# Projection steps of the next head pair, three per query block in the even head, and a fifth buffer for the first exponentials

## Chip, core and metric

The kernel runs on one core of a Trainium2 chip. The metric is the device time of one execution in microseconds (us). The engines are named as the profile names them: PE is TensorE's matmul, PEld its weight load, DVE is VectorE, ACT is ScalarE, POOL is GpSimd and SP issues most of the DMAs.

## What is computed

Two residual layers over 512 tokens of width 1024 in float32, each followed by a SwiGLU feed-forward. Layer 0 mixes tokens by stick-breaking attention, layer 1 by differential attention. The change lies in layer 1; cut to what matters, it is:

```python
def diff_mixer(h, positions, w_in, w_out, q_g, k_g, ..., sub_g, layer_idx):
    q, k, v = split(h @ w_in, 3)                  # 8 heads; q and k in 2 halves of 64, v of 128
    q, k = rms_norm(q, q_g), rms_norm(k, k_g)     # over each 64
    q1, q2, k1, k2 = partial_rope(...)            # the first 16 of each 64
    a = softmax(mask(q1 k1^T)) - lam * softmax(mask(q2 k2^T))
    o = rms_norm(a @ v, sub_g) * (1 - lam_init)   # per head
    return o @ w_out
```

## The kernel before

Activations are kept transposed, as eight tiles of 128 features by 512 tokens. Every matmul operand is split into a high and a low part, so one product is three matmuls (lines 216, 217 and 218). Layer 1's attention is `diff_layer`.

**Chunks and heads.** Heads go in pairs. Chunk c projects q, k and v of heads 2c and 2c+1. `qk_steps(c)` makes a tile of 512 columns for each of four token blocks in two steps each (8 steps of 12 matmuls of 512 columns), and `v_steps(c)` a tile of 256 columns in one step each (4 steps of 24 matmuls of 256 columns): 12 steps for a chunk. After its last block `qk_steps` normalises the whole chunk (L766 to L769) and applies the rotary part (L786 to L789). Each block's square (L758) goes to a scratch tile `tmp`, of which there are three, and so do the scratch of the rotary part and the square of `head_out` (L861).

**One head.** `head_stacks` transposes q and k of a head (L798) and splits them (L311 to L315; k's halves are doubled by a DMA from POOL, L334). `attend` then goes through four query blocks, the longest first: `weights(3)`, `weights(2)`, a bank of transposes (L358, then L361 and L362), `weights(1)`, a bank, `weights(0)`, a bank. `weights` makes two sets of scores (L340, L341), the maximum (L811), two exponentials (L812, tiles `e1` and `e2`) and combines them into `e1` (L824). All four `e1` tiles of a head are read by its last bank of transposes. Then `head` multiplies by v (tile `av`, L216 to L218), and `head_out` norms the head's output: L850, transposes L856 (`tn`), squares L861, the scaling L874, transposes L883 (`tb`) and the split L886, L887 into two tiles of pool `hp`. `head_out` of one head is called by the next one, after its `weights(3)`.

**Fillers.** The steps of chunks 1 to 3 stand in a queue; `attend` takes `counts[hd]` steps from it at four places of a head. In the middle of an odd head the rest of the next chunk's q and k is taken from the queue, and then `head_stacks` of the following head is called. From head 6 on, the queue holds `out_first`, which needs the outputs of heads 0 to 3 only; `out_second` needs those of heads 4 to 7 and follows the last head.

**What sets the order.** The kernel is built with `schedule_with_timeline_sim=True`: the build plays the program through in simulated time and writes each engine's queue in the order in which instructions became ready there, the earlier one in the program first where several are ready. So a filler step stands at one place in the program and may be run at another. Tiles of one tag take its buffers by turns, in program order. The rings that matter: `tmp` 3, `e1` 4, `e2` 2, scores in PSUM 2, projection tiles in PSUM (`mm`) 2, `wt_hi`/`wt_lo` 1, q2 and k2 stacks 2 each, v 2, pool `hp` 26 (the layer's input takes 16 of these, each head's output two).

Of the kernel before, what the change touches and what calls it, by code (L numbers as in the profile page):

```python
# [12 lines left out]
F32 = mybir.dt.float32  # L13
# [8 lines left out]
P = 128  # L22
S = 512
# [8 lines left out]
ROT = 16  # L32
RSQRT_MAGIC = float(0x5F3759DF)
TCK = dict(schedule_with_timeline_sim=True)
HP = 26
WB = 5
THIRDS = ((0, 8), (8, 8), (16, 6))
TWO_PI_A = 6.28125
# [5 lines left out]
def trunk(  # L44
# [30 lines left out]
    xp = ctx.enter_context(tc.tile_pool(name="xp", bufs=1))  # L75
    hp = ctx.enter_context(tc.tile_pool(name="hp", bufs=HP))
    wp = ctx.enter_context(tc.tile_pool(name="wp", bufs=WB))
# [199 lines left out]
    def out_first(layer, og):  # L277
        for g in range(4):
            w = out_load(layer, 0, g)
            for mi in range(2):  # L280
                m = g * 2 + mi
                ps = mm.tile([P, S], F32, tag="mm", name="ps_o")
                out_mms(ps, w, og, range(4), mi, 0, 3)
                V.tensor_tensor(x[m], x[m], ps, op=ALU.add)
                yield
# [51 lines left out]
    def scores(ps, q2, k2, e, qt):  # L337
        n = max(2, qt + 1) * P
        qs = slice(qt * P, (qt + 1) * P)
        T.matmul(ps[:, :n], q2[:, e, qs], k2[:, 0, e, :n], start=True, stop=False)  # L340
        T.matmul(ps[:, :n], q2[:, e, qs], k2[:, 1, e, :n], start=False, stop=True)  # L341
# [365 lines left out]
    def diff_layer(norm, nxt):  # L707
        h = norm.h
        with ExitStack() as st:
# [3 lines left out]
            at = st.enter_context(tc.tile_pool(name="at1", bufs=2))  # L713
# [88 lines left out]
            def weights(q2, k2, ss, qt):  # L802
                n = (qt + 1) * P
                nm = sm.tile([P, 2], F32, tag="nm", name="nm")
                e1 = at.tile([P, S], F32, tag="e1", bufs=4, name="e1")
                e2 = at.tile([P, S], F32, tag="e2", name="e2")
                for e, o in ((0, e1), (1, e2)):
                    ps = scp.tile([P, S], F32, tag="sc", name="sc")
                    scores(ps, q2, k2, e, qt)
                    V.memset(ps[0:64, n - 64 : n], NEG)  # L810
                    V.reduce_max(nm[:, e : e + 1], ps[:, :n], axis=AX.X, negate=True)  # L811
                    A.activation(  # L812
                        o[:, :n],
                        ps[:, :n],
                        AF.Exp,
                        bias=nm[:, e : e + 1],
                        accum_out=ss[:, e, qt : qt + 1],
                    )
                c = sm.tile([P, 2], F32, tag="c", name="c")
                V.reciprocal(c[:, 0:1], ss[:, 1, qt : qt + 1])  # L820
                V.tensor_scalar(
                    c[:, 1:2], ss[:, 0, qt : qt + 1], nlam, c[:, 0:1], op0=ALU.mult, op1=ALU.mult
                )
                V.scalar_tensor_tensor(  # L824
                    e1[:, :n], e2[:, :n], c[:, 1:2], e1[:, :n], op0=ALU.mult, op1=ALU.add
                )
                return e1

            def head(hh, q2, k2, v, after, middle, steps, before):
                ss = sm.tile([P, 2, TT], F32, tag="s12", name="s12")  # L830
                attend(tpp, wts, lambda qt: weights(q2, k2, ss, qt), after, middle, steps)
                before()
                v = v()
                av = avp.tile([P, S], F32, tag="av", name="av")
                hs = slice(hh * P, (hh + 1) * P)
                for kt in range(TT):
                    n, hi, lo = wt_chunk(wts, kt)
                    mm3(
                        av[:, :n],
                        (v[0][:, kt, hs], v[1][:, kt, hs]),  # L840
                        (hi, lo),
                        kt == 0,
                        kt == TT - 1,
                    )
                return av, ss
# [58 lines left out]
                gens["v", c] = v_steps(c, vs)  # L904
                fillers.extend((gens["qk", c], gens["v", c]))
            last = out_first(1, og)
            counts = ((2, 1, 2, 1), (2, 1, 1, 1)) * 3 + ((1, 1, 1, 1), (1, 1, 1, 1))
            for hd in range(8):
                hh = hd % 2
                c = hd // 2  # L910
# [32 lines left out]
    assert not todo  # L943
    n3 = Norm(gf, KT, True)
    diff_layer(n2, n3)
    ffn(1, n3, store)

# [72 lines left out]
```

## Time and profile before

| | before |
|---|---|
| median of 3 runs | 1301.82 us (1300.54 to 1305.36) |
| the profiled execution: its time | 1301.36 us |
| its span | 1299.6 us |
| PE busy | 1239.7 us (95%) |
| DVE busy | 740.2 us (57%) |
| ACT busy | 568.2 us (44%) |
| POOL busy | 80.8 us (6%) |
| chain that ended last, by engine | PE 90%, DVE 3%, ACT 3%, DMA 2% |

The page's second part cuts the span into 40 slices of 32.5 us. Layer 1's attention lies between about 640 and 931 us, slices 20 to 29. A head is recognised in the trace by its twelve `av` matmuls; the ends of these give the stretches in the rows below.

### The profile page before, as it was taken

The numbers are of one execution on the slowest core, as the hardware profiler recorded it, in microseconds if no ns is written. First come the engines' busy times: TensorE is split into PE (matmuls) and PEld (weight loads), VectorE is DVE, ScalarE is ACT, GpSimd is POOL, SyncE is SP. The second block draws the span as 40 slices with busy tenths as digits, with TensorE's granted clock in tenths as the row PEclk, the third lists the DMA queues.
The fourth block names the chain that finished last, engine by engine and source line by source line (L and its number), as shares of the span: only waits on it lengthen the run. The fifth ranks groups of instructions, "written<-read, shape, count | busy, mean of one in ns | idle before, by whom it ended". The sixth has DMA issues, their size and how long they took to land.

```text
span 1299.6 us, 16000 instructions
## 1 busy us (share of the span) xinstructions
PE 1239.7 (95%) x5974; PEld 1032.3 (79%) x5974; DVE 740.2 (57%) x1426; ACT 568.2 (44%) x964; POOL 80.8 (6%) x132
## 2 busy tenths in 40 slices
PE   6999999889999999999999997968899999999998
PEld 5888888778888888888888887745688888888886
DVE  5567868597544554455535657677754434443442
ACT  7777887455332432334324445345443223321220
POOL 1211111000000000000000000000000000000000
PEclk8999999999999999999999998979899999999999
DMA  7965768238776777766557352501222323332222
GB/s 222 220 148 134 169 143 191 58 97 275 247 227 244 242 246 231 243 233 227 196 194 227 131 158 90 174 17 33 97 100 97 95 97 98 98 97 97 93 73 77
DMA packets 61133, 199.44 MB, mean 153 GB/s; under 512 B 8320, under 2 KB 9344, under 8 KB 61056
## 3 DMA queue, kind: packets, MB, share of 16 engines
q1 hardware_dynamic: 42768, 140.74, 33.0%
q0 software_dynamic: 18144, 57.68, 16.8%
q8 instruction: 47, 0.77, 0.2%
q14 instruction: 30, 0.25, 0.1%
q10 hardware_dynamic: 144, 0.01, 0.0%
HBM read 154.36 MB, written 35.65 MB: 146 GB/s over the span
## 4 chain that ended last, share of the span: by engine, by line
PE 90%; DVE 3%; ACT 3%; DMA 2%; issue 1%; SPq 0%; POOL 0%; DVEq 0%; ACTq 0%; POOLq 0%
PE ps_d L217 6%; PE ps_d L216 6%; PE ps_d L218 6%; PE ps_g L218 6%; PE ps_g L216 6%; PE ps_g L217 6%; PE ps_u L218 6%; PE ps_u L216 6%; PE ps_u L217 6%; PE ps_nat L216 4%; PE ps_nat L217 4%; PE ps_nat L218 4%; PE ps_o L216 2%; PE ps_o L217 2%; PE ps_o L218 2%; PE tp L358 2%
## 5 line engine op out<-in xcount | busy, mean ns | idle before, releaser
L109 ACT ACTIVATE whi<-wraw 128x1024 fp32r<-128x1024 f32 (+1 forms) x136 | 138.6, 1033 | 355.8 <-PE ps_d L217 82.4
L110 DVE TENSOR_TENSOR wlo<-wraw,whi 128x1024 fp32r<-128x1024 f32 (+1 forms) x136 | 161.9, 1192 | 106.1 <-ACT whi L109 50.5
L217 PE MATMUL ps_d<-alo,whi 128*128 128x512 f32 x352 | 139.1, 396 | 0.0
L218 PE MATMUL ps_d<-ahi,wlo 128*128 128x512 f32 x352 | 139.0, 396 | 0.0
L216 PE MATMUL ps_d<-ahi,whi 128*128 128x512 f32 x352 | 138.9, 396 | 0.0
L216 PE MATMUL ps_u<-hhi,whi 128*128 128x512 f32 x352 | 137.7, 391 | 0.3 <-DVE x L298 0.2
L218 PE MATMUL ps_g<-hhi,wlo 128*128 128x512 f32 x352 | 137.6, 391 | 0.0
L217 PE MATMUL ps_g<-hlo,whi 128*128 128x512 f32 x352 | 137.2, 390 | 0.0
L218 PE MATMUL ps_u<-hhi,wlo 128*128 128x512 f32 x352 | 137.1, 390 | 0.0
L217 PE MATMUL ps_u<-hlo,whi 128*128 128x512 f32 x352 | 137.1, 390 | 0.0
L216 PE MATMUL ps_g<-hhi,whi 128*128 128x512 f32 x352 | 136.7, 390 | 0.0
L217 PE MATMUL ps_nat<-wlo,hhi 128*128 128x256 f32 (+1 forms) x384 | 124.7, 325 | 7.0 <-DMA wlo<-in_wv 7.0
L216 PE MATMUL ps_nat<-whi,hhi 128*128 128x256 f32 (+1 forms) x384 | 124.5, 326 | 1.1 <-DVE k L453 1.0
L218 PE MATMUL ps_nat<-whi,hlo 128*128 128x256 f32 (+1 forms) x384 | 124.7, 325 | 0.0
L606 DVE TENSOR_TENSOR x<-x,ps_d 128x512 f32<-128x512 f32 x48 | 32.8, 687 | 97.2 <-PE ps_d L218 97.1
L217 PEld LDWEIGHTS ps_nat<-wlo,hhi 128*128 128x128 f32 x384 | 74.1, 193 | 12.5 <-DMA wlo<-in_wv 7.2
L216 PEld LDWEIGHTS ps_nat<-whi,hhi 128*128 128x128 f32 x384 | 74.0, 193 | 7.0 <-DVE k L453 1.2
L217 PEld LDWEIGHTS ps_d<-alo,whi 128*128 128x128 f32 x352 | 66.2, 188 | 15.9
L218 PEld LDWEIGHTS ps_d<-ahi,wlo 128*128 128x128 f32 x352 | 66.2, 188 | 15.9
L216 PEld LDWEIGHTS ps_d<-ahi,whi 128*128 128x128 f32 x352 | 66.2, 188 | 15.9
L218 PEld LDWEIGHTS ps_nat<-whi,hlo 128*128 128x128 f32 x384 | 74.1, 193 | 5.1 <-issue 0.2
L216 PEld LDWEIGHTS ps_u<-hhi,whi 128*128 128x128 f32 x352 | 66.1, 188 | 14.9 <-ACT whi L109 0.6
(206 smaller groups left out, 2328.5 us busy)
## 6 DMA issues: line engine op xcount, KB each, us to landing
wraw<-in_wgu SPq DMA_DIRECT2D x88, 512.0 KB, 3.6
wraw<-in_wd SPq DMA_DIRECT2D x32, 512.0 KB, 3.6
k<-k POOLq DMA_DIRECT2D x32, 256.0 KB, 3.3
praw<-in_wqk SPq DMA_DIRECT2D x16, 512.0 KB, 5.7
kept_wqk<-whi POOLq DMA_DIRECT2D x16, 512.0 KB, 5.5
kept_wqk<-wlo POOLq DMA_DIRECT2D x16, 512.0 KB, 6.6
whi<-kept_wqk SPq DMA_DIRECT2D x16, 512.0 KB, 6.3
wlo<-kept_wqk SPq DMA_DIRECT2D x16, 512.0 KB, 5.9
```

The source lines that it names most:

```text
L109: A.activation(hi[:, :cols], raw[:, :cols], AF.Copy)
L110: V.tensor_tensor(lo[:, :cols], raw[:, :cols], hi.bitcast(F32)[:, :cols], op=ALU.subtract)
L216: T.matmul(ps, lh[0], rh[0], start=first, stop=False)
L217: T.matmul(ps, lh[0], rh[1], start=False, stop=False)
L218: T.matmul(ps, lh[1], rh[0], start=False, stop=last)
L358: T.transpose(tp[:, o : o + P], w[qt][:, kt * P : (kt + 1) * P], ident)
L606: V.tensor_tensor(x[m], x[m], ps, op=ALU.add)
```

## The change

```diff
-HP = 26
+HP = 25
...
             def weights(q2, k2, ss, qt):
                 n = (qt + 1) * P
                 nm = sm.tile([P, 2], F32, tag="nm", name="nm")
-                e1 = at.tile([P, S], F32, tag="e1", bufs=4, name="e1")
+                e1 = at.tile([P, S], F32, tag="e1", bufs=5, name="e1")
...
-            counts = ((2, 1, 2, 1), (2, 1, 1, 1)) * 3 + ((1, 1, 1, 1), (1, 1, 1, 1))
+            counts = ((3, 3, 3, 3), (0, 0, 0, 0)) * 3 + ((1, 1, 1, 1), (1, 1, 1, 1))
```

Before, six steps are taken in an even head and five in an odd one, so the last steps of a chunk spill into the odd head and, from there, into the next even head. After the change the even head 2c takes all 12 steps of chunk c+1 and the odd head takes none. `e1` has five buffers instead of four, and pool `hp` 25 tiles instead of 26 (a tile of either is 2 KB per partition). No instruction is added or removed.

## Rows read from the trace of the kernel before

**Rows 1.** The page, parts 1 and 2: engines, and PE's clock by slice
```profile
PE 1239.7 (95%) x5974; PEld 1032.3 (79%) x5974; DVE 740.2 (57%) x1426; ACT 568.2 (44%) x964; POOL 80.8 (6%) x132
PEclk8999999999999999999999998979899999999999
```

**Rows 2.** Busy by stretch: length, PE, PEld, DVE, ACT, POOL, clock, DMA, GB/s
```profile
721.70:743.60 21.90, 21.90 (x134) 19.39 (x134) 14.70 (x56) 9.59 (x27) 0.00 (x0) 1.00 0.50 181
743.60:788.10 44.50, 44.50 (x273) 39.72 (x272) 25.58 (x73) 20.86 (x55) 2.31 (x4) 1.00 0.53 171
788.10:802.50 14.40, 8.85 (x38) 6.71 (x36) 12.52 (x52) 7.07 (x24) 0.00 (x0) 0.64 0.00 1
802.50:846.20 43.70, 39.62 (x214) 32.58 (x214) 32.00 (x87) 18.44 (x49) 2.32 (x4) 1.00 0.45 145
846.20:863.30 17.10, 11.27 (x44) 7.85 (x43) 15.24 (x62) 7.58 (x25) 0.00 (x0) 0.70 0.01 1
863.30:894.60 31.30, 20.91 (x89) 15.24 (x88) 22.55 (x68) 16.44 (x45) 2.31 (x4) 0.84 0.17 34
894.60:905.90 11.30, 9.12 (x51) 6.85 (x50) 8.29 (x36) 5.99 (x21) 0.00 (x0) 1.00 0.12 26
905.90:931.00 25.10, 19.60 (x76) 15.42 (x75) 13.61 (x30) 12.21 (x24) 0.00 (x0) 0.80 0.22 74
```

**Rows 3.** PE in order of time: scores at two head boundaries (start, length)
```profile
728.40 0.28 PE L341 MATMUL sc<-k,q 128*128 128x256 f32 x1
...
751.61 0.39 PE L340 MATMUL sc<-k,q 128*128 128x512 f32 x1
...
839.36 0.28 PE L341 MATMUL sc<-k,q 128*128 128x256 f32 x1
...
840.90 0.50 PE L340 MATMUL sc<-k,q 128*128 128x512 f32 x1 [0.93 <-ACT e L812]
```

**Rows 4.** ACT in order of time: chunk 1's last block and head 0's squares
```profile
694.42 0.69 ACT L756 ACTIVATE qk_nat<-ps_nat,rstd 128x512 f32<-128x512 f32 x1
...
727.67 0.37 ACT L861 ACTIVATE o_sq<-tn,rs 128x128 f32<-128x128 f32 x1
...
728.01 0.64 ACT L758 ACTIVATE qk_sq<-qk_nat 128x512 f32<-128x512 f32 x1
```

**Rows 5.** DVE in order of time: chunk 1's norm
```profile
733.92 2.28 DVE L769 TENSOR_TENSOR qk_nat<-qk_nat,rs_u 128x2048 f32<-128x2048 f32 x1
```

**Rows 6.** ACT in order of time: the first two v blocks of chunk 3
```profile
802.44 0.84 ACT L735 ACTIVATE v1h<-ps_nat,rsv 128x256 fp32r<-128x256 f32 x2 [2.12 <-PE av L217]
```

**Rows 7.** ACT in order of time: an exponential of head 1's first block
```profile
713.19 0.69 ACT L812 ACTIVATE e<-sc,nm 128x512 f32<-128x512 f32 x1 [0.21 <-PE tp L358]
```

**Rows 8.** Groups of DVE by form, 689 to 906 us: count, busy us, mean ns
```profile
L811 DVE TENSOR_REDUCE nm<-sc 128x1 f32<-128x512 f32 x16 | 10.9, 689 | 0.4
L315 DVE SCALAR_TENSOR_TENSOR q<-tqk,gqT,q 64x512 fp32r<-64x512 f32 x14 | 10.5, 750 | 7.0 <-ACT q L314 6.5
L312 DVE TENSOR_TENSOR k<-tqk,k 64x512 fp32r<-64x512 f32 x14 | 9.6, 684 | 2.4 <-ACT k L311 2.0
L824 DVE SCALAR_TENSOR_TENSOR e<-e,c,e 128x512 f32<-128x512 f32 x8 | 5.9, 742 | 0.3
```

**Rows 9.** PE in order of time: matmuls of chunk 0's projections
```profile
654.72 0.39 PE L217 MATMUL ps_nat<-wlo,hhi 128*128 128x512 f32 x1
...
657.66 0.39 PE L218 MATMUL ps_nat<-whi,hlo 128*128 128x512 f32 x1
657.89 0.28 PE L216 MATMUL ps_nat<-whi,hhi 128*128 128x256 f32 x1
...
669.28 0.28 PE L218 MATMUL ps_nat<-whi,hlo 128*128 128x256 f32 x1
```

**Rows 10.** DVE and PE in order of time, layer 0: pair 4's output, last projection
```profile
187.05 0.69 DVE L533 TENSOR_TENSOR olo<-o,ohi 128x512 fp32r<-128x512 f32 x1
...
190.67 0.39 PE L216 MATMUL ps_k<-hhi,whi 128*128 128x512 f32 x1
```

## Prediction

> **What bounds the kernel now.** The page comes first: PE is busy for 95% of the span, and its clock is full except in the first slice and in slices 25 to 29 [rows 1]. So the rest of the kernel has little to give, and I look at layer 1's attention alone, by stretches that end with each head's product with v [rows 2]. The reader should see two halves. Up to 788.1 (the end of head 2) PE is busy without a gap at full clock. From there on it isn't: head 3 takes 14.4 us with PE busy 8.85 at clock 0.64, and heads 4 to 7 take 43.7, 17.1, 31.3 and 11.3 us, 103.4 in all, with PE busy 80.9. DVE is busy for 12.52 of head 3's 14.4 us (87%) and 15.24 of head 5's 17.1 (89%), but for 78.1 of the whole 103.4 (75.5%).
>
> The lengths say where to look: an odd head ends soon after its even partner, and an even head long after the odd one before it. The next view is PE in order of time, scores alone [rows 3]. From head 1's last score at 728.40 to head 2's first at 751.61 no score runs for 23 us; between heads 4 and 5 it is 1.5 us. There are three such odd-to-even boundaries, all of 21 to 25 us, and the even-to-odd ones that I read take 3 us at most. What is late at an odd-to-even boundary is the next chunk's stacks of q and k. Chunk 1's last block is evacuated at 694.42, but its square runs at 728.01, straight after head 0's four output squares, the last of which starts at 727.67 [rows 4]; the norm of the chunk follows at 733.92 [rows 5]. The squares of the chunk and of `head_out` share the three `tmp` tiles, and these are handed out in program order. Before the change the chunk's last steps stand in the odd head, behind the even head's `head_out`, so its norm waits for that head to end, although its matmuls were done 33 us earlier. Chunks 2 and 3 show the same.
>
> The second stop is the v ring: chunk 3's first two v blocks are evacuated at 802.44, when head 3's product has released a buffer [rows 6]. Until then they hold both projection tiles in PSUM, no further filler can start, and head 3 runs bare.
>
> **Part 1, the counts.** It adds and removes nothing. All 12 steps of a chunk now stand in the even head, ahead of that head's `head_out`. Chunk 1's norm no longer waits for any head and can follow its last block by about the time that it took after 728.01, that is at about 700 instead of 733.92. Chunks 2 and 3 come behind the previous odd head's `head_out` instead of the next even one's: earlier by one head. So the stacks of heads 2, 4 and 6 should be ready when the odd head before them makes its last scores, and the 21 to 25 us without scores should shrink towards the 1.5 of an even-to-odd boundary. Three such gaps would be over 60 us of the chain, but this isn't the gain: next in line are PE up to head 3 and DVE after it.
>
> *Up to head 3.* PE is full until 788.1, so an earlier head 2 only changes what PE does when. Head 3's own work of 8.85 us at clock 0.64 is 5.7 us at full clock [rows 2]. If heads 2 and 3 keep up with the fillers, head 3 ends at 793.8 instead of 802.5: **8.7 us**. The least is 0 (head 3 still runs bare), the most is this, since the chunk's v still can't pass head 3.
>
> *Heads 4 to 7.* DVE has 78.1 us to do. Head 4's stacks (2 x 0.750 + 2 x 0.684) and its first block (2 x 0.689 + 0.742) [rows 8] move ahead into the part that PE bounds, where DVE was busy for 25.58 of 44.5 us: 5.0 us less, 73.1 left. At the 89% of head 5 this takes 82.1 us, at the 75.5% of now 96.8, against 103.4: a gain of 6.6 to 21.3. I take 84%, nearer to head 5, since the late stacks were the largest thing that kept DVE waiting there, but not at it, since `out_first` fills PE between the heads: 87.0 us, a gain of **16.4 us**. PE's share is 74.2 us at full clock (39.62 + 0.70 x 11.27 + 0.84 x 20.91 + 9.12), so it fits too. The last 25.1 us, head 7's output and `out_second`, stay.
>
> Moved with the steps are their DMAs: 12 weight loads per chunk on SP and the k copies on POOL (16 in all). Their order among themselves doesn't change, POOL is idle for most of the stage [rows 2], and SP's loads still come as the weight ring allows: cost 0 as long as the loads run ahead; if that cover went, up to a load's latency per chunk, which the range holds. On DVE, the chunk's norm now stands ahead of the even head's later blocks, and these and the bank of transposes behind them wait for it (2.28 us for its longest instruction [rows 5]). In heads 0 and 2 PE's fillers cover that; in head 4 it is inside the 84%.
>
> **Part 2, the fifth e1 buffer.** An exponential of head 1's first block starts 0.21 us after the last transposes of head 0 [rows 7]: with four buffers a head's first `e1` waits for the previous head's last bank. The fifth removes this wait once per head. It is worth between 0 (in the stretch that PE fills) and, for each of heads 4 to 7, the 1.5 us of an even-to-odd boundary [rows 3], 6 us; I count it in the 84% and not again.
>
> **Part 3, hp with 25 tiles.** In layer 0, pair 4's second output tile now needs the layer's first input tile back, which the last k projection frees. That projection's first matmul is at 190.67, the output's split at 187.05 [rows 10]: 4 us later for a tile that is read only by `out_second`. Cost 0, at most these 4 us if DVE's queue behind it waits. In layer 1 the same holds for head 4's second tile, which comes after the last projection.
>
> **Sum:** 8.7 + 16.4 = 25.1 us off the profiled execution's 1301.36 (which is 0.5 below the median): 1276.
>
> Here a rule of the Trainium skill bears on the first term. PE is full by its matmuls, while its weight loads fill 39.72 of 44.5 us [rows 2]. Perfetto Trace Analysis (Identifying the Most-Contended Engine) says that matmul busy time is no good measure and that the weight loads' share is; by that rule 11% of the stretch is still to be had, an estimate of 5 us more in those 44.5. The trace speaks against it: matmuls of 512 columns start 0.226 us apart (2.94 us for 13) with no wait between them [rows 9].
>
> **Rivals.** *Slower.* Program order could bind: the projections stay in the even head where they are written, and odd heads run with nothing beside them. A chunk is 96 matmuls at 0.226 and 96 at 0.120 (11.39 for 95) [rows 9], 33.2 us; an even head of 33.2 + 7.9 (head 5's PE work at full clock, 0.70 x 11.27) takes 41. With head 0 done at 721.7 as now, heads 2 and 4 at 41 and five bare heads at X, half of `out_first` left over (48 x 0.226 = 10.8) and the last 25.1, the stage ends at 839.6 + 5X, against 931. It decides at X = 18.3. Bare heads took 14.4 and 17.1, head 1 under fillers 21.9 [rows 2]. At 21.9 the end is 949, at 19.5 it is 937, 6 us later: 1307, and up to 1319. Against it: chunk 3's first v blocks are done and waiting when head 3 ends [rows 6], though they stand in head 5, so the build does pull projections ahead. The skill's Perfetto Trace Analysis (Optimization Strategy) sides with this rival: it advises to interleave regimes that load different engines, which the change undoes.
>
> *A part only.* The weight tiles `wt_hi` and `wt_lo` have one buffer, so a head's transposes wait for the previous head's product. If that chain binds heads 4 to 7, only the first term comes: 1301.4 - 8.7 = 1292.7.
>
> *No change.* If the build already runs each step when it is ready and the late norm only fills time that PE or DVE need anyway, 1301.
>
> *More.* DVE without a gap in heads 4 to 7: 73.1 us, a gain of 30.3 + 8.7 = 39, so 1262.
>
> **How the numbers follow.** The forecast has 0.45 and by itself spans 1268 to 1286; a part only 0.20; more 0.07; no change 0.13; slower 0.15. The range reaches from 1260 over the forecast, the part and no change to 1300, and leaves out the slower case and a little below. Half a per cent, 6.5 us, is about what a measurement of this kernel can tell from no change: faster by more 0.72, within 0.13, slower 0.15.
>
> **What would show it.** Right: chunk 1's norm (L769) near 700, and chunk 2's and 3's ahead of their even head's output squares; scores of heads 2, 4 and 6 within about 5 us of the odd head's last; head 3's product ending near 794; heads 4 to 7 in about 87 us with DVE near 84%. Wrong: the norms still behind the even head's squares (no change); PE idle in head 1 (slower); odd-to-even gaps of scores gone, but the heads no shorter (a part only).

## Result and profile after

| | before | after |
|---|---|---|
| median (4 runs each) | 1301.55 us | 1270.19 us (1269.10 to 1273.07) |
| ratio, 95% interval | | 0.9757 [0.9732, 0.9783] |
| the profiled execution: its time | 1301.36 us | 1270.67 us |
| its span | 1299.6 us | 1268.9 us |

The kernel is faster by 2.4%, some 31 us, where 25 were forecast. The engines' lines of the page and PE's clock, which answer to [rows 1]:

```profile
PE 1227.1 (97%) x5974; PEld 1024.4 (81%) x5974; DVE 736.1 (58%) x1426; ACT 567.1 (45%) x964; POOL 80.7 (6%) x132
PEclk9999999999999999999999999999999999999999
```

The work is the same (5974 matmuls, DVE 736 us), and PE's clock stays at nine tenths or more in the mean of every slice; by stretch it still falls, to 0.81 in head 6 and 0.86 in the tail. Busy time by stretch, with the columns of [rows 2]. The first line runs from the layer's first sum of squares to head 3's product, then come heads 4, 5, 6 and 7, the tail, and at last heads 4 to 7 in one:

```profile
644.30:796.50 152.20, 151.88 (x916) 134.61 (x915) 95.77 (x297) 70.56 (x172) 5.82 (x10) 1.00 0.51 168
...
796.50:827.20 30.70, 26.82 (x158) 22.39 (x156) 28.24 (x95) 16.05 (x47) 1.16 (x2) 1.00 0.39 130
827.20:845.60 18.40, 18.40 (x103) 15.71 (x102) 15.16 (x46) 10.08 (x27) 1.16 (x2) 1.00 0.45 144
845.60:863.20 17.60, 14.31 (x64) 10.58 (x64) 16.12 (x59) 10.84 (x36) 1.16 (x2) 0.81 0.15 30
863.20:876.00 12.80, 10.54 (x60) 8.37 (x60) 8.73 (x38) 6.66 (x23) 0.00 (x0) 1.00 0.10 23
876.00:900.20 24.20, 18.71 (x75) 14.79 (x74) 12.71 (x28) 10.90 (x22) 0.00 (x0) 0.86 0.24 76
796.50:876.00 79.50, 70.07 (x380) 57.05 (x378) 68.27 (x236) 43.63 (x132) 3.47 (x6) 0.96 0.31 94
```

The same stretches of the kernel before, to compare the first and the last line with:

```profile
642.70:802.50 159.80, 154.14 (x902) 135.45 (x900) 90.70 (x282) 66.66 (x164) 4.67 (x8) 0.97 0.47 158
...
802.50:905.90 103.40, 80.92 (x392) 62.52 (x392) 78.07 (x252) 48.45 (x140) 4.63 (x8) 0.90 0.26 74
```

Up to head 3's end 7.6 us are saved (159.8 to 152.2), in heads 4 to 7 23.9 (103.4 to 79.5), in the tail 0.9; the layer started 1.6 us later. That is 30.8, and the spans differ by 30.7. PE is now full up to head 3 (151.88 of 152.20).

The chunks' norms, DVE in order of time, against [rows 5]. The second stands ahead of head 2's first output square, which starts at 777.57, the third ahead of head 4's at 832.19:

```profile
703.96 2.29 DVE L769 TENSOR_TENSOR qk_nat<-qk_nat,rs_u 128x2048 f32<-128x2048 f32 x1
...
763.66 2.28 DVE L769 TENSOR_TENSOR qk_nat<-qk_nat,rs_u 128x2048 f32<-128x2048 f32 x1
...
813.03 2.28 DVE L769 TENSOR_TENSOR qk_nat<-qk_nat,rs_u 128x2048 f32<-128x2048 f32 x1
```

And ACT, chunk 1's last square and then the first square of head 0's output, against [rows 4]; the square no longer waits for the head:

```profile
696.75 0.64 ACT L758 ACTIVATE qk_sq<-qk_nat 128x512 f32<-128x512 f32 x1
...
734.97 0.37 ACT L861 ACTIVATE o_sq<-tn,rs 128x128 f32<-128x128 f32 x1 [1.90 <-PE tn L856]
```

The three odd-to-even boundaries, PE's scores in order of time, against [rows 3]. In each pair the first line is the odd head's last score and the second, of 512 columns, the even head's first. From head 1 to head 2, 23 us without a score have become less than 1. From head 3 to 4 and from 5 to 6, 24.9 and 22.0 us have become 8.3 and 7.2, so these gaps are shorter but not gone. They cost PE next to nothing: it is busy for 8.09 of the 8.30 us from 783.90 on and for all of the 7.10 from 834.90 on.

```profile
735.57 0.28 PE L341 MATMUL sc<-k,q 128*128 128x256 f32 x1
736.40 0.48 PE L340 MATMUL sc<-k,q 128*128 128x512 f32 x1
...
783.89 0.28 PE L341 MATMUL sc<-k,q 128*128 128x256 f32 x1
...
792.16 0.50 PE L340 MATMUL sc<-k,q 128*128 128x512 f32 x1 [0.21 <-DMA k<-k]
...
834.86 0.28 PE L341 MATMUL sc<-k,q 128*128 128x256 f32 x1
...
842.03 0.48 PE L340 MATMUL sc<-k,q 128*128 128x512 f32 x1
```

### The profile page after: what moved, and what is told of

Read it like the earlier page. It is cut to its first block, busy times and chain, and to the rows that moved or that the text cites. A ratio compares the mean times of both kernels' runs of the same rounds, so it can differ in the third digit from the quotient of the medians.

```text
span 1268.9 us, 15987 instructions
## 1 busy us (share of the span) xinstructions
PE 1227.1 (97%) x5974; PEld 1024.4 (81%) x5974; DVE 736.1 (58%) x1426; ACT 567.1 (45%) x964; POOL 80.7 (6%) x132
## 4 chain that ended last, share of the span: by engine, by line
PE 89%; DMA 4%; DVE 3%; ACT 3%; issue 1%; SPq 0%; DVEq 0%; ACTq 0%
PE ps_d L218 6%; PE ps_d L216 6%; PE ps_d L217 6%; PE ps_g L218 6%; PE ps_g L216 6%; PE ps_u L218 6%; PE ps_u L216 6%; PE ps_g L217 6%; PE ps_u L217 6%; PE ps_nat L216 4%; PE ps_nat L217 4%; PE ps_nat L218 4%; PE ps_o L216 2%; PE ps_o L217 2%; PE ps_o L218 2%; PE tp L358 2%
## 5 line engine op out<-in xcount | busy, mean ns | idle before, releaser
L587 DVE TENSOR_TENSOR g<-ps_g,rbc 128x512 f32<-128x512 f32 x44 | 30.3, 690 | 84.6 <-PE ps_g L218 81.1
```

Of the source, the lines that this page charges most:

```text
L587: V.tensor_tensor(g32, pg, norm.bc, op=ALU.mult)
```

## Experiments

Theory going in: scratch tiles are handed out in program order, so the next chunk's norm waited for the even head's output; the counts put it ahead. Each run's expectation stands as it was written before it.

**Which part of the change does it.** `counts_only` is the kernel before with the new counts:

```diff
-            counts = ((2, 1, 2, 1), (2, 1, 1, 1)) * 3 + ...
+            counts = ((3, 3, 3, 3), (0, 0, 0, 0)) * 3 + ...
```

> Only the counts are changed; e1 keeps four buffers and hp 26 tiles. Theory (the scratch ring holds back the next chunk's norm, and the counts free it): nearly the whole gain, 1270 to 1278 us, with chunk 1's norm (L769) near 704 as in the changed kernel. Rival A (the fifth e1 buffer lets heads overlap, the counts only shift the fillers): at most a third of the gain, 1290 us or more.

Measured: 1269.76 us, ratio to the kernel before 0.9759 [0.9736, 0.9782]. This is the whole gain. Chunk 1's L769 is at 700.40.

`bufs_only` is the other part:

```diff
-HP = 26
+HP = 25
...
-                e1 = at.tile([P, S], F32, tag="e1", bufs=4, name="e1")
+                e1 = at.tile([P, S], F32, tag="e1", bufs=5, name="e1")
```

> The old counts; e1 with five buffers and hp with 25 tiles. Theory: 1296 to 1302 us, since the next chunk's norm stays behind the even head's squares (chunk 1's L769 near 734). Rival A (the e1 buffer): 1270 to 1290 us.

Measured: 1312.14 us, 1.0082 [1.0067, 1.0097]. Rival A falls, and so does the price that I gave: with the old counts the buffers cost 10 us. `hp25_only` splits them:

```diff
-HP = 26
+HP = 25
```

> The kernel before with hp at 25 tiles and nothing else. It splits bufs_only (1312 us, 10 over the kernel before) into its two buffers. Theory (the tile of hp costs nothing, as predicted; the fifth e1 buffer lets an odd head's work come ahead of an even one's and costs the 10 us with the old counts): 1300 to 1304 us. Rival F (the missing hp tile holds back head 4's output): 1306 us or more.

Measured: 1300.98 us, 0.9992 [0.9980, 1.0005]. The hp tile costs nothing, so it is the fifth e1 buffer that costs when the norms are late. Why is not settled. The odd-to-even gaps without scores are longer in `bufs_only`, 31.4, 31.6 and 26.3 us against 23.2, 24.9 and 22.0 before. One piece of this is seen on PE, at head 4's first score, which waits 4.63 us for the copy of k's halves (0.40 us before, at 819.01):

```profile
822.87 0.77 PE L340 MATMUL sc<-k,q 128*128 128x512 f32 x1 [4.63 <-DMA k<-k]
```

**Is it the scratch, or where the filler steps stand?** `own_scratch` keeps the old counts and gives a chunk's squares and rotary part a buffer of their own:

```diff
-HP = 26
+HP = 25
...
-                    sq = tmp.tile([P, S], F32, tag="tmp", name="qk_sq")
+                    sq = tmp.tile([P, S], F32, tag="qsq", bufs=1, name="qk_sq")
...
-                    mt = tmp.tile([P, S], F32, tag="tmp", name="rope")
+                    mt = tmp.tile([P, S], F32, tag="qsq", bufs=1, name="rope")
```

> The old counts and four e1 buffers; the squares and the rotary scratch of a chunk (qk_sq, rope) get one buffer of their own instead of the three that they share with head_out's squares; hp has 25 tiles to make room. Theory (it is the ring): the norm of a chunk runs when its last block is done although its steps still stand in the odd head, and the time is 1270 to 1282 us. Rival B (what counts is where the filler steps stand, their number beside each head): 1297 us or more.

Measured: 1303.91 us, 1.0020 [1.0008, 1.0032]. By its expectation rival B was right. The trace says otherwise. ACT ran the chunk's last square at 694.41 now, and DVE in order of time shows the first step of the norm (L766) behind it. The next step, the first of `rsqrt` (L142), comes 32.6 us later, straight behind the same step for head 0's output, and L769 36 us later:

```profile
696.30 0.16 DVE L766 TENSOR_SCALAR qk_ss<-qk_ss 128x32 f32<-128x32 f32 x1
...
728.91 0.14 DVE L142 TENSOR_SCALAR rs_u<-o_ss 128x4 int32<-128x4 int32 x1
728.95 0.18 DVE L142 TENSOR_SCALAR rs_u<-qk_ss 128x32 int32<-128x32 int32 x1
...
732.53 2.28 DVE L769 TENSOR_TENSOR qk_nat<-qk_nat,rs_u 128x2048 f32<-128x2048 f32 x1
```

Between L766 and L769 stands only `rsqrt`, whose two small tiles `rs_u` and `rs_t` also belong to rings that `head_out` uses: a second pair of shared rings behind the first. These rings have four buffers each (pool `sm`). No `rs_u` is in use between chunk 0's L769, at 663.31, and 728.91, and from then on the head's and the chunk's are in use side by side. So the chunk did not wait for a free buffer: its tile comes behind head 0's in program order, and was handed out only after it. `own_both` separates these as well, still with the old counts (the lines of `own_scratch` for `qk_sq` and `rope` are in it too):

```diff
-HP = 26
+HP = 24
...
-    def rsqrt(v, n):
-        u = sm.tile([P, 32], F32, tag="rs_u", name="rs_u")[:, :n]
-        t = sm.tile([P, 32], F32, tag="rs_t", name="rs_t")[:, :n]
+    def rsqrt(v, n, own=""):
+        u = sm.tile([P, 32], F32, tag="rs_u" + own, name="rs_u")[:, :n]
+        t = sm.tile([P, 32], F32, tag="rs_t" + own, name="rs_t")[:, :n]
...
-                u = rsqrt(ss, 32)
+                u = rsqrt(ss, 32, "c")
...
```

> As own_scratch (old counts, four e1 buffers, a buffer of their own for a chunk's squares and rotary scratch), and also own small tiles for the reciprocal root of a chunk's norm (tags rs_u and rs_t apart from those of head_out); hp has 24 tiles to make room. Theory (own_scratch left one of the shared rings: its squares ran early, but L769 still stood at 732.5, behind the root of head 0's output): chunk 1's L769 comes before 715 and the time is 1268 to 1282 us, without any change of the counts. Rival B (the place of the filler steps beside the heads): 1297 us or more, as own_scratch.

Measured: 1271.55 us, 0.9774 [0.9759, 0.9789]. Not a count is changed and the gain of the change is there but for a microsecond or two; L769 follows L766 by 6 us:

```profile
696.95 0.16 DVE L766 TENSOR_SCALAR qk_ss<-qk_ss 128x32 f32<-128x32 f32 x1
...
703.14 2.29 DVE L769 TENSOR_TENSOR qk_nat<-qk_nat,rs_u 128x2048 f32<-128x2048 f32 x1
```

So the order in which the shared rings hand out their tiles is the cause, and the counts are one way round it. Separating the small tiles alone was not run.

**From the other side: how many steps, or on which side of the head.** `rope_spill` and `rope_in` are the changed kernel with other counts. They differ by one step of twelve, which decides whether the ninth call, the one that normalises the chunk, stands in the even or in the odd head. This is `rope_spill`; `rope_in` has ((2, 2, 2, 3), (1, 1, 1, 0)):

```diff
-            counts = ((3, 3, 3, 3), (0, 0, 0, 0)) * 3 + ...
+            counts = ((2, 2, 2, 2), (1, 1, 1, 1)) * 3 + ...
```

> The changed kernel with counts (2,2,2,2) in an even and (1,1,1,1) in an odd head: all eight q and k steps stand in the even head, the four v steps in the odd one, and the rotary part of the chunk, which is called by the step after the eighth, comes behind the even head's output squares again. Theory: the chunk's squares and norm (L769) are early, but its rotary part (L786 to L789) waits in the ring for the even head's squares; the stacks of heads 2, 4 and 6 are late by about half as much as before, and the time is 1280 to 1295 us. Rival B (filler steps beside each head; two thirds of the change made): 1268 to 1278 us.

Measured: 1308.07 us, 1.0050 [1.0034, 1.0066]. Slower than I expected, and L769 is late, which I had expected only of the rotary part (both are in the ninth call). This kernel also has the fifth e1 buffer, so with late norms the kernel to set it against is `bufs_only`, at 1312.14 us. Here too the squares and L766 are early (697.38), and the root waits.

```profile
697.38 0.18 DVE L766 TENSOR_SCALAR qk_ss<-qk_ss 128x32 f32<-128x32 f32 x1
...
732.52 2.29 DVE L769 TENSOR_TENSOR qk_nat<-qk_nat,rs_u 128x2048 f32<-128x2048 f32 x1
```

> The changed kernel with counts (2,2,2,3) and (1,1,1,0): one step more in the even head than in rope_spill and one less in the odd head, so that the call of the ninth step, which normalises the chunk, falls into the even head. Theory (the norm must stand ahead of the even head's output): chunk 1's L769 near 704 and 1268 to 1278 us. Rival B (filler steps beside each head, which differ by one of twelve from rope_spill's 1308): 1298 to 1310 us.

Measured: 1275.43 us, 0.9804 [0.9786, 0.9821], L769 at 702.48. One step moved is worth 33 us; rival B would have it worth a twelfth of the change. The 5 us by which `rope_in` stays behind the changed kernel were not looked into.

**What sets heads 4 to 7.** `dve_late` and `dve_early` are `counts_only` with hp 25 and one more multiply behind every block of heads 4 to 7 (`hd >= 4`) or 0 to 3 (`hd < 4`):

```diff
+                if hd >= 4:
+                    V.tensor_tensor(junk, junk, junk, op=ALU.mult)
                 return e1
```

> The new counts with four e1 buffers and hp 25, and one more multiply of 128x512 (about 0.69 us, on a tile of its own, read by nobody) on DVE behind each of the 16 blocks of heads 4 to 7: 11 us of DVE in all. Theory (DVE sets heads 4 to 7 after the change, 68 of 79.5 us busy): 7 to 11 us over counts_only, 1277 to 1281 us. Rival C (these heads wait for their own chain of scores, exponentials and transposes, and DVE has room): 0 to 4 us over it.

> The same 16 multiplies behind the blocks of heads 0 to 3, where PE is full. Theory (PE sets this part): 0 to 3 us over counts_only, 1270 to 1273 us. Rival D (DVE's work delays the heads there too, and head 3's end moves): 6 us or more over it.

Measured: 1272.12 us (0.9777 [0.9761, 0.9793]) and 1271.25 us (0.9783 [0.9760, 0.9806]). Neither tests anything: the multiplies wait for nothing, and the build placed them in layer 0's feed-forward, at 298 to 333 us in one and 297 to 332 in the other. From DVE in order of time of `dve_late`:

```profile
298.23 0.69 DVE L830 TENSOR_TENSOR junk<-junk 128x512 f32<-128x512 f32 x1
```

`dve_tied` makes each depend on its block:

```diff
-                    V.tensor_tensor(junk, junk, junk, op=ALU.mult)
+                    V.scalar_tensor_tensor(
+                        junk, junk, c[:, 1:2], junk, op0=ALU.mult, op1=ALU.mult
+                    )
```

> In dve_late the multiplies depended on nothing, and the build placed them at 298 to 333 us, in the feed-forward of layer 0: it tested nothing. Here each of the 16 (0.74 us, 11.9 in all, DVE) reads the scalar of its block in heads 4 to 7, so it can't run before that block, and nobody waits for its result. New counts, four e1 buffers, hp 25. Theory (DVE sets heads 4 to 7): 8 to 12 us over counts_only's 1269.8, so 1278 to 1282 us. Rival C (DVE has room there; the chain of each head or PE sets them): 0 to 4 us over it.

Measured: 1279.57 us, 0.9827 [0.9813, 0.9842], 9.8 us over `counts_only`. `chain_late` puts less work on DVE, but in the way of each block:

```diff
+                if hd >= 4:
+                    V.scalar_tensor_tensor(
+                        e1[:, :n], e1[:, :n], 1.0, e1[:, :n], op0=ALU.mult, op1=ALU.max
+                    )
                 return e1
```

> New counts with four e1 buffers and hp 26; in heads 4 to 7 each combined block e1 goes through DVE once more before its transposes (0.74, 0.59, 0.46 and 0.35 us for the four widths, 8.6 us in all), so the same engine has less extra work than in dve_tied, but on the path of every block. Theory (DVE sets these heads, by its sum): about 0.7 of what dve_tied shows, 6 to 9 us over counts_only. Rival C (the chain of each head sets them): as much as dve_tied or more.

Measured: 1278.49 us, 0.9823 [0.9803, 0.9843], 8.7 us over `counts_only`. `pe_more` adds a fourth product to `out_first` in layer 1, low by low:

```diff
-            mm3(ps, (w[0][:, c], w[1][:, c]), og[kk], kk == first, kk == last)
+            if layer == 1:
+                T.matmul(ps, w[1][:, c], og[kk][1], start=kk == first, stop=False)
+            mm3(ps, (w[0][:, c], w[1][:, c]), og[kk], kk == first and layer == 0, kk == last)
...
```

> New counts with four e1 buffers and hp 26; out_first of layer 1 also multiplies the two low parts, 32 matmuls of 512 columns (7.2 us of PE at 0.226) in heads 4 to 7. Theory (PE has 70 of 79.5 us there and DVE binds): 0 to 4 us over counts_only. Rival E (PE sets heads 4 to 7 too): 6 to 8 us over it.

Measured: 1282.07 us, 0.9844 [0.9829, 0.9858], 12.3 us over `counts_only` for 7.2 us of matmuls. The stretch of heads 4 to 7, columns as in [rows 2], in `counts_only`, `dve_tied`, `chain_late` and `pe_more`; in all four it is taken from 1.2 to 1.3 us behind the end of head 3's product to 0.6 to 0.7 us behind that of head 7's:

```profile
794.50:874.00 79.50, 70.07 (x376) 56.60 (x377) 68.54 (x237) 43.94 (x132) 3.47 (x6) 0.98 0.30 93
```

```profile
798.00:887.70 89.70, 77.82 (x376) 61.89 (x377) 77.77 (x252) 44.36 (x133) 3.49 (x6) 0.89 0.28 83
```

```profile
797.10:883.40 86.30, 73.53 (x376) 59.33 (x377) 73.03 (x253) 44.75 (x133) 3.49 (x6) 0.92 0.27 84
```

```profile
798.40:890.10 91.70, 81.38 (x423) 67.96 (x424) 69.87 (x237) 43.54 (x133) 3.49 (x6) 0.94 0.26 81
```

The multiplies by their own durations, from the groups of DVE by line in `dve_tied` and `chain_late` (columns as in [rows 8], the last one idle time before):

```profile
L830 DVE SCALAR_TENSOR_TENSOR junk<-junk,c 128x512 f32<-128x512 f32 x16 | 11.9, 744 | 0.0
```

```profile
L828 DVE SCALAR_TENSOR_TENSOR e<-e 128x512 f32<-128x512 f32 x4 | 2.7, 678 | 0.0
L828 DVE SCALAR_TENSOR_TENSOR e<-e 128x384 f32<-128x384 f32 x4 | 2.2, 545 | 0.0
L828 DVE SCALAR_TENSOR_TENSOR e<-e 128x256 f32<-128x256 f32 x4 | 1.6, 405 | 0.0
L828 DVE SCALAR_TENSOR_TENSOR e<-e 128x128 f32<-128x128 f32 x4 | 1.1, 279 | 0.0
```

In `dve_tied` 11.9 us of multiplies whose result nobody reads lengthen the stretch by 10.2; in `chain_late` 7.6 us in the way of each block lengthen it by 6.8. So DVE doesn't have the room that rival C gives it. More than this the two runs don't tell:

- They don't tell work on the chain of a block from work beside it. By these stretches, of one execution each, a microsecond of instruction costs 0.86 in `dve_tied` and 0.89 in `chain_late`; by the medians of four executions, 9.8 and 8.7 us, it costs 0.82 and 1.14. The four executions of `counts_only` alone lie 6 us apart, and over `dve_late`, the same kernel but for where its multiplies run, `dve_tied` takes only 7.5 us more.
- A multiply that nobody reads is still in the way on DVE itself: behind 15 of the 16 the next instruction of DVE starts within 0.1 us, as one does that had been waiting. So this run doesn't show that DVE's sum sets the pace either.
- PE's granted clock falls as well, from 0.98 to 0.89 and 0.92. PE is busy for 77.82 us in `dve_tied` and for 70.07 in `counts_only` with the same 376 matmuls, so a part of the added time may be PE's.

Rival E, that PE sets the pace, holds beside it. In `pe_more` the stretch grows by 12.2 us for 32 added matmuls, 7.2 us at 0.226. Part of the difference is seen in the groups of PE in that stretch, first of `counts_only`, then of `pe_more`:

```profile
L216 PE MATMUL ps_o<-ohi,whi 128*128 128x512 f32 x44 | 17.8, 420 | 1.2 <-DVE x L284 0.4 <-ACT ohi L886 0.3 <-ACT e L812 0.2
```

```profile
L216 PE MATMUL ps_o<-ohi,whi 128*128 128x512 f32 x49 | 19.1, 414 | 1.9 <-ACT e L814 1.9
L276 PE MATMUL ps_o<-olo,wlo 128*128 128x512 f32 x32 | 13.1, 408 | 1.5 <-DVE olo L889 1.3 <-DVE v1l L738 0.2
```

All 32 ran in the stretch, and fifteen more of the output's own matmuls (x49 against x44, and the same for the two other products) came into it from the tail: 15 x 0.226 = 3.4 us. The tail, up to the first matmul of the next feed-forward, got only 0.9 us shorter for that (22.9 us from 874.00 on, 22.0 from 890.10 on). The last 1.6 us (12.2 - 7.2 - 3.4) stay open; PE's clock is 0.94 there against 0.98. With PE busy for 70.07 and DVE for 68.54 of 79.5 us in `counts_only`, most of what is added to either engine shows in the time. Neither is full, so the pace may also be that of each block's chain, which runs through both; these runs don't separate DVE's sum, PE's sum and the chain.

## Why the prediction was right

*The late stacks, and their cause.* Right as a mechanism: L769 near 704 where 700 was said, and the three norms ahead of their even head's output. The gaps of scores were to fall to about 5 us or less; they fell to 0.8, 8.3 and 7.2, so this sign failed at two of three boundaries, where PE was full with other work. The name of the ring was half of it. I read the `tmp` ring from [rows 4], where the chunk's square follows head 0's squares without a gap, and did not ask whether the next step of the norm is held as well. It is, by `rs_u` and `rs_t`, which the list of rings ahead of the prediction leaves out; `own_scratch`, which removes only what I named, gains nothing, and `own_both` gains nearly all. That the counts put the chunk's whole norm ahead, and so got round the rings that I had not named as well, is why the half reading cost the forecast nothing; that part was luck.

*Up to head 3:* 8.7 forecast, 7.6 measured. The term was built on PE being full until the fillers end, and it is, 151.88 of 152.20 us.

*Heads 4 to 7:* 16.4 forecast from a span of 6.6 to 21.3, 23.9 measured. This is the mis-sized term, and the measured gain lies outside its span; the forecast of the whole was still near, 25 us for 31. The share came out near: DVE is busy for 68.27 of 79.5 us, 86% where I took 84. In the term's own measure, what I sized wrongly is the work that leaves the stretch. I moved head 4's stacks and its first block, 5.0 us; in fact DVE's busy time fell by 9.8 (78.07 to 68.27). The groups of DVE in both stretches say what left: head 4's stacks and half of head 5's (the splits of q from x8 to x4 and those of k from x8 to x6, 4.4 us), and chunk 2's rotary part (2.8 us). The first block did not leave, but for one of its two maxima (0.6 us): L824 is there x16 in both. The rest of the 2.6 us that remain is spread over small groups and the overlap of records. From the groups of DVE in the stretch before, and then after:

```profile
L315 DVE SCALAR_TENSOR_TENSOR q<-tqk,gqT,q 64x512 fp32r<-64x512 f32 x8 | 6.0, 750 | 3.3 <-ACT q L314 2.9
L312 DVE TENSOR_TENSOR k<-tqk,k 64x512 fp32r<-64x512 f32 x8 | 5.5, 686 | 2.0 <-ACT k L311 1.8
```

```profile
L312 DVE TENSOR_TENSOR k<-tqk,k 64x512 fp32r<-64x512 f32 x6 | 4.1, 685 | 0.1
L315 DVE SCALAR_TENSOR_TENSOR q<-tqk,gqT,q 64x512 fp32r<-64x512 f32 x4 | 3.0, 750 | 0.1
```

At 84%, 4.8 us more are 5.7 of the 7.5 by which the term was short, and the share makes up the rest. That DVE's smaller sum is what made the stretch shorter is argued and not shown. I had put PE down as merely fitting (74.2 of 87.0), but `pe_more` shows that work added to PE costs at least as much as work added to DVE, and PE's own busy time fell as much as DVE's, by 10.9 us (80.92 to 70.07), with 12 matmuls less and at a clock of 0.96 instead of 0.90.

*The last stretch* was left as it was: 25.1 to 24.2.

*The fifth e1 buffer* was priced from 0 upward and counted inside the 84%. With the new counts it is worth nothing that can be measured (1270.19 with it, 1269.76 without), and with the old ones it costs 10 us. The bound should have reached below zero: no row excluded a loss, for instance from letting one head's work come ahead of another's. It did no harm to the sum only since the counts came with it. *The hp tile* costs nothing, as said.

*The rivals.* The slower one, program order binding with bare odd heads, did not come: PE is full through heads 1 and 3 of the changed kernel (19.40 of 19.40 us from 730.00 on, 23.48 of 23.70 from 772.80 on), because the build pulls later chunks' projections into them. The Trainium skill's advice in Perfetto Trace Analysis (Optimization Strategy) to interleave regimes, which sided with it, is met here by the build and not by the counts. The weight-load measure of the Trainium skill (Perfetto Trace Analysis, Identifying the Most-Contended Engine) promised room up to head 3; PEld there is 134.61 of 152.20 us after and 135.45 of 159.80 before, so the rise from 85% to 88% is the removed idle time, and PE's matmuls leave no gap. The rival of a part only would have stopped at 1292.7, and the stretch of heads 4 to 7 refutes it.

## What to carry to other kernels

Where scratch tiles of one tag are handed out in program order, a step that is written behind a late consumer of the same tag waits for it, whatever its own inputs: look for an instruction that starts straight behind an unrelated one of another stage, long after its own input. A ring with free buffers can hold a step back in this way, as `rs_u` did with four. Check every ring on that step's way, and not only the first, since freeing one alone may gain nothing. An added load in an experiment has to depend on the place that it is to load, or the build will put it where it costs nothing.

## What the runs showed that I had not expected

The copies of k's halves took very different times from issue to landing. For head 4's two copies it was 4.0 and 3.6 us in the kernel before, 8.9 and 8.1 in `bufs_only`, where PE waited for them for 4.63 us, and 8.6 and 9.5 in the changed kernel, where PE had other work and waited for 0.21. The traces show what goes with it. SP's last four weight loads ahead of the first copy were issued 3.8 to 5.7 us ahead of it in the kernel before, and 0.8 to 3.0 us in `bufs_only`; in the changed kernel eight were issued from 2.0 us ahead of it to 3.5 us behind it. In these three kernels the copies that had no load issued within 8 us of them landed in 2.9 to 3.1 us. No run moved the loads to test it.
